# A decoder layer on one core: seven block products in the down projection of three token blocks, DeltaNet scalings moved to ScalarE, and two changes to the order of the work

## The chip, the cores and the metric

One core of a Trainium2 chip runs the whole program. The metric is the device time of one execution, in microseconds (us); lower is better. The kernel before was timed in three runs: median 2986.15 us, from 2983.44 to 2987.88.

The core has a matrix engine (TensorE, PE in the profile; its weight loads are listed apart as PEld), VectorE (DVE), ScalarE (ACT), GpSimd (POOL), and SyncE (SP), whose queue issues every transfer of this kernel.

## The reference, cut to what matters

```python
def decoder_layer(x, ...):
    y = parallel_mixer(rms_norm(x, norm_mix), ...)      # Conformer convolution | gated DeltaNet, then w_out
    x = x + y
    x = x + memory_attend(rms_norm(x, norm_mem_q), mem_k, mem_v, w_mq, w_mo)
    x = x + swiglu(rms_norm(x, norm_ffn), w_gate, w_up, w_down)
    return x, ...

def swiglu(h, w_gate, w_up, w_down):
    return (jax.nn.silu(h @ w_gate) * (h @ w_up)) @ w_down
```

There is one layer, a prompt of 2048 tokens, eight single decode tokens, a model width of 1024 and an FFN width of 2816. Everything is float32. The down projection multiplies a 2048x2816 activation by a 2816x1024 weight.

## The kernel before, in words

**Layout.** Channels lie on the 128 partitions and tokens along the free dimension. The prompt is cut into four blocks of 512 tokens (`NB`, `TB`). The FFN width is 22 tiles of 128 channels (`NF`), taken as 11 pairs (`NG`); the model width is 8 tiles (`KC`). The decode tokens ride along: in the FFN they are added to block 2 (`DEC_F`), whose token halves are therefore 260 wide and not 256.

**Float32 in three passes.** A number is split into a rounded upper part and the rest. `three` issues three matmuls for one weight tile: upper times upper, upper weight times lower operand, lower weight times upper operand. Each matmul instruction brings its own weight load.

**Weights.** `WS` streams them. `load` issues a transfer into one of 11 `raw` tiles (`NRAW`); `split` makes a `w` tile of two parts from it, with a copy on ACT and a subtraction on POOL or DVE, into one of 6 slots (`NW`). `engine` chooses POOL if the planner's clock says that POOL will be free soon enough, else DVE. The plan (`plan`) lists in advance which tile is used when. A tile that is already split in DRAM (`sums`) is loaded straight into its slot.

**The FFN of a block.** `ffn_steps` lists the steps. For each tile `f` of the FFN width, gate and up are computed together as a 2x2 block product over two halves of the contraction and two halves of the tokens, with seven products instead of eight (`Q1 P5 P6 Q2 Q3 Q7 P4`): each product is 12 matmuls, 256 tokens wide (260 in block 2). Four of the seven weights are sums of blocks. Block 0 computes the sums, splits them and writes them to DRAM (`sums`); blocks 1 to 3 load them from there. Products share PSUM banks by a letter (x, y, z; tiles `fx`, `fy`, `fz`): a later product adds to what an earlier one left in the bank, and an engine reads the bank in between. `ff_split` multiplies the two results and splits the product on ACT and DVE into an `act` tile (`ff`); there are 22 such tiles (`NACT`), and 14 of them hold the operands of gate and up during a block.

**The down projection.** `down(g, j)` takes a pair of FFN tiles `g` and two of the eight output tiles: 2 outputs x 2 tiles x 3 passes = 12 matmuls of 512 tokens (tile `dn`), from one weight tile; in block 2, 24 matmuls of 260. Four such steps, one before `P4` and three after it, finish a pair. Each output is then added to the residual `x` on DVE (`add_x`, `add_half`). Block 2 leaves three pairs (`HOLD`) to `rest`, which runs while the operands of block 3 are made; block 3 ends in `last`, in two halves of the tokens, followed by the final norm.

**The rest.** Before the FFNs, the first 1200 us or so hold the input projection, the convolution and the DeltaNet of all blocks (`dn_front`, `dn_chain`), the memory keys and values, and the output and attention parts of blocks 0 and 1; those of blocks 2 and 3 come after the FFNs of blocks 0 and 1. `square_gemm` does the projections with a square weight. For `w_out` in block 0 it begins with two output tiles at once, in the other blocks with four, and takes the remaining output tiles one by one.

**What sets the order.** Two planners. While the program is written down, `Sched` and `Clock` run a list of lanes against estimated costs; here POOL or DVE is chosen, and tiles get their slots. `Engine` estimates each ACT, DVE and POOL instruction. Then `Tape.order` puts every instruction of every engine in its final order: at each point the free engine takes, of its instructions whose inputs are ready by the estimated times, the one that is due first. That order is fixed; the engines then run it and wait for each other by semaphores.

Every instruction is issued by a helper, so all rows of the profile name one line (L469); rows are told apart by their tiles.

## Time and profile before

| | |
|---|---|
| median of three runs | 2986.15 us |
| the profiled execution | 2990.62 us |
| its span, first to last instruction | 2988.8 us |
| mean granted TensorE clock | 0.994 of full speed |
| matmul instructions | 18972 |
| PE busy | 2932.8 us (98%) |
| DVE busy | 2002.1 us (67%) |
| POOL busy | 1478.9 us (49%) |
| ACT busy | 1312.1 us (44%) |
| moved by DMA | 593.89 MB, 199 GB/s |

A row of a group names the line, the engine, the operation, the tile written and the tiles read, and how many; then the busy time of all, the mean of one in ns, and the idle time before them with what ended it. A row of the timeline gives the start, the length and the same names. Since matmuls are pipelined, the length of one (about 280 ns at 256 columns) is not its cost in a run: that is the distance from the start of one run to the start of the next, divided by the number of matmuls. Rows of the windows view give each engine's busy time in a stretch, the granted clock, the DMA engines' busy share and the rate.

### The profile page before, as it was taken

The numbers are of one execution on the slowest core, as the hardware profiler recorded it, in microseconds if no ns is written. First come the engines' busy times: TensorE is split into PE (matmuls) and PEld (weight loads), VectorE is DVE, ScalarE is ACT, GpSimd is POOL, SyncE is SP. The second block draws the span as 40 slices with busy tenths as digits, with TensorE's granted clock in tenths as the row PEclk, the third lists the DMA queues.
The fourth block names the chain that finished last, engine by engine and source line by source line (L and its number), as shares of the span: only waits on it lengthen the run. The fifth ranks groups of instructions, "written<-read, shape, count | busy, mean of one in ns | idle before, by whom it ended". The sixth has DMA issues, their size and how long they took to land. (4 is left out here: it accounts for less than half of the span.)

```text
span 2988.8 us, 53327 instructions
## 1 busy us (share of the span) xinstructions
PE 2932.8 (98%) x18972; PEld 2609.6 (87%) x18972; DVE 2002.1 (67%) x4105; ACT 1312.1 (44%) x2672; POOL 1478.9 (49%) x1403
## 2 busy tenths in 40 slices
PE   9999999999999999999999999999999999999998
PEld 7998878887888887899988789988888999999997
DVE  8758897987755757998788974433675444664345
ACT  6533455444654344545544553333453233333233
POOL 3544554786554654457776124445413444344444
PEclk9999999999999999999999999999999999999999
DMA  6533425777663425766768767867526666666664
GB/s 213 157 102 99 138 93 173 256 236 249 222 222 117 131 82 195 234 196 212 268 252 268 247 216 244 268 220 241 185 91 227 208 226 215 212 239 220 216 224 136
DMA packets 361963, 593.89 MB, mean 199 GB/s; under 512 B 54017, under 2 KB 148545, under 8 KB 361681
## 3 DMA queue, kind: packets, MB, share of 16 engines
q1 hardware_dynamic: 361696, 590.47, 59.9%
q8 instruction: 151, 2.47, 0.3%
q14 instruction: 116, 0.94, 0.1%
HBM read 476.65 MB, written 114.27 MB: 198 GB/s over the span
## 5 line engine op out<-in xcount | busy, mean ns | idle before, releaser
L469 POOL TENSOR_TENSOR w<-raw,w 128x512 fp32r<-128x512 f32 x713 | 962.3, 1359 | 891.1 <-ACT w L469 842.3
L469 ACT ACTIVATE w<-raw 128x512 fp32r<-128x512 f32 x912 | 569.7, 631 | 905.2 <-PE fx L469 183.7
L469 PE MATMUL dn<-ff,w 128*128 128x512 f32 (+2 forms) x2688 | 518.1, 348 | 3.9 <-ACT ffs L469 2.6
L469 PEld LDWEIGHTS dn<-ff,w 128*128 128x128 f32 x2688 | 422.1, 188 | 64.7 <-ACT ffs L469 2.8
L469 PE MATMUL fy<-op,w 128*128 128x256 f32 (+1 forms) x3168 | 428.5, 283 | 4.7 <-DMA w<-sums 3.2
L469 PEld LDWEIGHTS fy<-op,w 128*128 128x128 f32 x3168 | 400.5, 189 | 10.4 <-DVE ffu L469 3.0
L469 PE MATMUL hd<-hT,w 128*128 128x512 f32 (+2 forms) x1920 | 396.7, 358 | 9.1 <-ACT w L469 5.9
L469 DVE SCALAR_TENSOR_TENSOR cacc<-cu,cw,cacc 128x512 f32<-128x512 f32 x480 | 358.2, 746 | 9.0 <-ACT cacc L469 3.8
L469 PEld LDWEIGHTS hd<-hT,w 128*128 128x128 f32 x1920 | 306.3, 190 | 54.6 <-ACT w L469 6.6
L469 DVE TENSOR_TENSOR x<-dn,x 128x512 f32<-128x512 f32 (+1 forms) x448 | 254.1, 571 | 129.2 <-PE dn L469 126.3
L469 PE MATMUL fz<-op,w 128*128 128x256 f32 (+1 forms) x2112 | 287.0, 283 | 1.0 <-DMA w<-sums 0.9
L469 PE MATMUL fx<-op,w 128*128 128x256 f32 (+1 forms) x2112 | 285.3, 283 | 1.0 <-DVE ffs L469 0.9
L469 PEld LDWEIGHTS fx<-op,w 128*128 128x128 f32 x2112 | 268.3, 189 | 7.8 <-issue 1.2
L469 PEld LDWEIGHTS fz<-op,w 128*128 128x128 f32 x2112 | 265.8, 189 | 3.7 <-issue 2.6
L469 POOL TENSOR_TENSOR sqj<-sqj,sqj 128x512 f32<-128x512 f32 (+1 forms) x98 | 134.9, 1376 | 255.7 <-ACT sqj L469 253.3
L469 DVE TENSOR_TENSOR w<-raw,w 128x512 fp32r<-128x512 f32 x199 | 167.2, 845 | 59.8 <-ACT w L469 55.8
L469 PE MATMUL sc<-w,hT 128*128 128x512 f32 x768 | 190.2, 399 | 3.2 <-DVE w L469 1.7
L469 PE MATMUL rg<-catS,w 128*128 128x512 f32 (+2 forms) x960 | 189.4, 353 | 0.0
L469 PE MATMUL rg<-pT,w 128*128 128x512 f32 x768 | 188.9, 399 | 0.4 <-ACT pT L469 0.4
L469 DVE TENSOR_TENSOR ffu<-fy,ffu 128x256 f32<-128x256 f32 (+1 forms) x176 | 74.3, 422 | 164.1 <-PE fy L469 163.7
L469 PEld LDWEIGHTS rg<-catS,w 128*128 128x128 f32 x960 | 154.4, 188 | 24.4 <-ACT jn L469 0.2
L469 PEld LDWEIGHTS sc<-w,hT 128*128 128x128 f32 x768 | 141.6, 188 | 37.5 <-DVE w L469 2.6
(378 smaller groups left out, 4089.6 us busy)
## 6 DMA issues: line engine op xcount, KB each, us to landing
w<-sums SPq DMA_DIRECT2D x296, 512.0 KB, 4.4
raw<-in_w_gate_dram SPq DMA_DIRECT2D x192, 256.0 KB, 3.2
sums<-w SPq DMA_DIRECT2D x88, 512.0 KB, 4.1
raw<-in_w_down_dram SPq DMA_DIRECT2D x176, 256.0 KB, 3.3
raw<-in_w_up_dram SPq DMA_DIRECT2D x118, 256.0 KB, 3.0
raw<-in_w_in_dram SPq DMA_DIRECT2D x96, 256.0 KB, 3.0
raw<-in_w_out_dram SPq DMA_DIRECT2D x64, 256.0 KB, 3.1
raw<-wk SPq DMA_DIRECT2D x64, 256.0 KB, 2.8
```

The costliest lines, as they stand in the source:

```text
L469: fn(*args, **kw)
```

## The change

**Seven products in the down projection** of blocks 1 to 3, for the first ten of the eleven pairs. A pair of FFN tiles, the outputs `j` and `j + 4`, and the two token halves make a 2x2 block product. `downs(g, j)` does two pairs at once: seven products of 2 pairs x 3 passes = 6 matmuls each, 256 (260) wide, so 42 matmuls and four weight tiles a step. `pair_split` makes the sums of the activations on DVE and splits them into four `act` tiles for a pair (3.5 tiles' worth of elements) where there were two. In block 1 `sums_down` makes the sums of the weights with four 128-column instructions on POOL or DVE and writes both weight tiles unsplit to DRAM (`dsums`); blocks 2 and 3 load them and split them. The columns of `w_down` are laid out for this on the host. The steps stand in pairs around `P4` of two FFN tiles in four. In block 2, `x` now holds the decode columns beside the others, so that one addition does both.

```diff
+DS_B = 1
+NDS = 5
+DS_AT = ((1, 0), (1, 1), (2, 0), (2, 1))
...
+    def ffn_steps_ds(b):
+        steps = []
+        for f in range(NF):
...
+            steps += [("Q2", f), ("Q3", f), ("Q7", f)]
+            units = [[], []]
+            for g in range(NDS - (b == NB - 2)):
+                for j, (df, end) in enumerate(DS_AT):
+                    if f == min(4 * g + 4 + df, NF - 1):
+                        units[end].append(("downs", g, j))
+            early = not units[0] + units[1] and f + 1 < NF
+            if early:
+                steps.append(("Q1", f + 1))
+            steps += units[0] + [("P4", f)] + units[1]
...
+    def downs_plan(b, g, j):
+        if b > DS_B:
+            for n in range(2):
+                for p in (2 * g, 2 * g + 1):
+                    plan.append(("dsums", "s", (p, j), n))
+            return
+        raws = {}
+        for p in (2 * g, 2 * g + 1):
+            for n in (1, 0):
+                raws[p, n] = plan.raw("dma", "w_down", "h", (p, j), n)
...
+        def sums_down(self, at, r0, r1):
+            (a11, a12, s1, s2), (s3, s4, a22, a21) = ([r[:, n * P : (n + 1) * P] for n in range(4)] for r in (r0, r1))
+            eng = self.engine(2600.0)
+            for out, x, y, op in (
+                (s1, a21, a22, ALU.add), (s2, s1, a11, ALU.subtract), (s3, a11, a21, ALU.subtract), (s4, a12, s2, ALU.subtract)
+            ):
+                eng.tensor_tensor(out=out, in0=x, in1=y, op=op)
+            p, j = at
+            dma(wsrc["dsums"][p, j, 0], r0)
+            dma(wsrc["dsums"][p, j, 1, :, : 3 * P], r1[:, : 3 * P])
...
+        def pair_split(p):
+            (u1, s1), (u2, s2) = prod.pop(2 * p), prod.pop(2 * p + 1)
+            half = lambda t, n: t[:, n * w : (n + 1) * w]
+            yield [u2, s2]
+            V.tensor_tensor(out=u2, in0=u2, in1=s2, op=ALU.mult)
+            V.tensor_tensor(out=half(s2, 1), in0=half(u2, 1), in1=half(u1, 1), op=ALU.subtract)
+            V.tensor_tensor(out=half(u1, 1), in0=half(u1, 1), in1=half(u1, 0), op=ALU.subtract)
+            V.tensor_tensor(out=half(s2, 0), in0=half(u2, 1), in1=half(u1, 1), op=ALU.subtract)
+            V.tensor_tensor(out=half(s1, 0), in0=half(u2, 0), in1=half(s2, 0), op=ALU.subtract)
+            for n, (src, wd) in enumerate(((u1, 2 * w), (u2, 2 * w), (s2, 2 * w), (s1, w))):
+                yield ("act", 1)
+                a = act("fo")
+                A.activation(out=a[:, 0, :wd], in_=src[:, :wd], func=AF.Copy)
+                yield a
+                V.tensor_tensor(out=a[:, 1, :wd], in0=src[:, :wd], in1=a[:, 0, :wd].bitcast(F32), op=ALU.subtract)
...
+        def downs(g, j):
+            ps_ = (2 * g, 2 * g + 1)
+            S.until(lambda: all((p, n) in hx for p in ps_ for n in range(4)), "ff")
+            wts, bk = {}, {}
+            for n, at, (x, h), t, m, half in (
+                (0, 0, (0, 0), "x", j, 0), (0, 1, (1, 0), "y", j, 0), (0, 2, (0, 1), "z", j + 4, 1), (0, 3, (2, 0), "x", j, 1),
+                (1, 1, (1, 1), "z", j, 1), (1, 0, (2, 1), "x", j + 4, 1), (1, 2, (3, 0), "x", j + 4, 0),
+            ):
...
+                first = t not in bk
+                if first:
+                    bk[t] = pm("d" + t, (P, w))
+                pt = bk[t]
+                for p in ps_:
+                    wt = wts[n, p]
+                    three([pt], wk(wt, 0, at), wk(wt, 1, at), hx[p, x], [(h * w, (h + 1) * w)], first and p == ps_[0], p == ps_[1], True)
+                    tick()
...
+                V.tensor_tensor(out=xs[m][:, lo:hi], in0=pt, in1=xs[m][:, lo:hi], op=ALU.add)
```

The letter in `downs` is the PSUM bank: the seven products go to x, y, z, x, z, x, x in this order, and after each one DVE reads its bank into the residual.

**Small DeltaNet scalings on ScalarE**: five DVE instructions become ACT instructions, and the last of them becomes four.

```diff
-        V.tensor_copy(
-            out=t16.rearrange("p (i j) -> p i j", j=16), in_=w16[:, 0:256].rearrange("p (j i) -> p i j", i=16)
+        A.activation(
+            out=t16.rearrange("p (i j) -> p i j", j=16), in_=w16[:, 0:256].rearrange("p (j i) -> p i j", i=16), func=AF.Copy
...
-        V.tensor_scalar(out=u1[64:P], in0=pu[64:P], scalar1=-1.0, scalar2=None, op0=ALU.mult)
+        A.activation(out=u1[64:P], in_=pu[64:P], func=AF.Copy, scale=-1.0)
...
-        V.tensor_copy(out=W[0:64, :, 64:P], in_=pu)
+        A.activation(out=W[0:64, :, 64:P], in_=pu, func=AF.Copy)
...
-            V.tensor_scalar(out=vv, in0=pc[:, 1, :], scalar1=brk[:, c : c + 1], scalar2=None, op0=ALU.mult)
+            A.activation(out=vv, in_=pc[:, 1, :], func=AF.Copy, scale=brk[:, c : c + 1])
...
-        V.tensor_tensor(out=osc, in0=po, in1=bc(fc, 2, [P, NT, DK]), op=ALU.mult)
+        for c in range(NT):
+            A.activation(out=osc[:, c, :], in_=po[:, c, :], func=AF.Copy, scale=fc[:, c : c + 1])
```

**Shared port in the list's clock**: the first planner's clock now lets a POOL instruction and a DVE instruction with two SBUF inputs start only one after the other.

```diff
+            port = self.name == "pool" or self.name == "dve" and sum(a.space != bass.MemoryType.PSUM and elems(a) > 1 for a in ins) > 1
+            if port:
+                self.clock.at[self.name] = max(self.clock.at[self.name], self.clock.port)
+            t = self.clock.run(self.name, ns, ins, out)
+            if port:
+                self.clock.port = t + ns
```

**Paired output tiles**: `square_gemm` begins `w_out` with two output tiles in every block, and the weight is loaded in the form that block 0 used.

```diff
-        square_plan("w_out", CAT, b == 0)
+        square_plan("w_out", CAT, True)
...
-        n0 = 2 if dec else 4
+        two = w == "w_out"
+        n0 = 2 if two else 4
```

More of the change, by code (lines that the diff above doesn't have):

```diff
@@ L975, in split, with split_down @@
             self.used(k)
+        def split_down(self, j, k, r, t):
+            _, _, at, n = plan[j]
+            wd = TB - n * P
+            if plan.raws[k][2] == "h" and n == 0:
+                self.sums_down(at, r, self.raw[k - 1])
+            A.activation(out=t[:, 0, :wd], in_=r[:, :wd], func=AF.Copy)
+            self.engine().tensor_tensor(out=t[:, 1, :wd], in0=r[:, :wd], in1=t[:, 0, :wd].bitcast(F32), op=ALU.subtract)
+            self.tiles[j] = t
+            self.sp += 1
+            self.used(k)
+        def sums_down(self, at, r0, r1):
[8 more added lines that the diff above has]
+            dma(wsrc["dsums"][p, j, 1, :, : 3 * P], r1[:, : 3 * P])
         def ready(self, k):
+            if 0 <= k < self.ld and plan.raws[k][2] == "h" and plan.raws[k][4] == 0 and C.when([self.raw[k - 1]]) > S.vt:
+                return False
             return k < 0 or k < self.ld and C.when([self.raw[k]]) <= S.vt
@@ L2234, in square_gemm @@
         for m in range(n0):
-            if m == n0 - 1:
-                S.until(lambda: any(C.bank_free(t) < 1e12 for t in ("mm", *others())), "fourth bank")
-            pts.append([pm("rg", (P, hi - lo), others() if len(spans) * m + k > 2 else []) for k, (lo, hi) in enumerate(spans)])
+            pts.append([])
+            for k, (lo, hi) in enumerate(spans):
+                lent = lambda: others() if len(spans) * m + k > 2 else []
+                S.until(lambda: any(C.bank_free(t) < 1e12 for t in ("mm", *lent())), "fourth bank")
+                pts[m].append(pm("rg", (P, hi - lo), lent()))
         for n_, kc in enumerate(order):
-            if not dec:
+            if not two:
                 wt = ws.get(w, "r", kc, 0)
@@ L2252, in square_gemm @@
                 tick()
-            if not dec:
+            if not two:
                 ws.free(1)
@@ L2725, in rest @@
         def rest():
-            for g in range(NG - HOLD, NG):
-                for j in range(KC // 2):
-                    down(g, j)
+            for j in range(KC // 2):
+                downs(NDS - 1, j)
+            for j in range(KC // 2):
+                down(NG - 1, j)
             if b == DEC_F:
```

100 lines of the change are left out of this document (79 added, 21 removed).

## The prediction, made before the change was run

> **What bounds the kernel now.** I read the page's busy times first, then the stages in the windows view, then what PE waited for.
>
> ```profile
> PE 2932.8 (98%) x18972; PEld 2609.6 (87%) x18972; DVE 2002.1 (67%) x4105; ACT 1312.1 (44%) x2672; POOL 1478.9 (49%) x1403
> ```
> ```profile
> 300.00:600.00 300.00, 296.17 (x1673) 245.37 (x1673) 263.33 (x567) 148.78 (x313) 165.21 (x197) 0.99 0.51 165
> 600.00:900.00 300.00, 287.21 (x1706) 246.59 (x1705) 213.97 (x407) 161.94 (x320) 193.01 (x185) 0.99 0.71 231
> ```
> ```profile
> 1230.00:1600.00 370.00, 366.52 (x2632) 335.97 (x2631) 316.96 (x584) 180.92 (x390) 251.24 (x229) 1.00 0.69 234
> ...
> 1786.00:2118.00 332.00, 329.00 (x2293) 301.71 (x2292) 146.28 (x257) 117.78 (x223) 157.96 (x120) 1.00 0.74 247
> ...
> 2288.00:2598.00 310.00, 308.65 (x2564) 308.11 (x2563) 148.05 (x429) 99.60 (x193) 135.76 (x99) 1.00 0.70 228
> ...
> 2640.00:2957.00 317.00, 315.80 (x2241) 295.85 (x2240) 135.12 (x233) 99.51 (x191) 140.61 (x104) 1.00 0.67 224
> ```
>
> In a windows row the columns after the length are PE, PEld, DVE, ACT, POOL, the granted clock, the DMA share and GB/s. The last four rows are the FFNs of blocks 0 to 3. In those of blocks 1 to 3 PE is busy for 329.00 of 332, 308.65 of 310 and 315.80 of 317 us, at the full clock, while DVE, ACT and POOL are under half busy. So matmul time sets the end, and a matmul removed there is a matmul's time gained until something else is late. What PE waited for, in the whole span, says how little that is now:
>
> ```profile
> PE fy L469 <- DMA w<-sums: 3.2, 4, 1.5
> ...
> PE dn L469 <- ACT ffs L469: 2.6, 1, 2.6
> ```
>
> The busy time of a pipelined group is not its cost, so I take the pace from starts of neighbouring runs in the timeline, once for 512 columns and once for 260:
>
> ```profile
> 1518.47 2.95 PE L469 MATMUL dn<-ff,w 128*128 128x512 f32 x12
> 1521.26 1.58 PE L469 MATMUL fy<-op,w 128*128 128x256 f32 x12
> 1522.68 8.55 PE L469 MATMUL dn<-ff,w 128*128 128x512 f32 x36
> 1531.07 1.58 PE L469 MATMUL fx<-op,w 128*128 128x256 f32 x12
> 1532.49 1.58 PE L469 MATMUL fz<-op,w 128*128 128x256 f32 x12
> ```
> ```profile
> 2309.72 3.11 PE L469 MATMUL dn<-ff,w 128*128 128x260 f32 x24
> 2312.67 1.60 PE L469 MATMUL fy<-op,w 128*128 128x260 f32 x12
> 2314.11 8.80 PE L469 MATMUL dn<-ff,w 128*128 128x260 f32 x72
> 2322.75 1.62 PE L469 MATMUL fx<-op,w 128*128 128x260 f32 x12
> 2324.20 1.61 PE L469 MATMUL fz<-op,w 128*128 128x260 f32 x12
> ```
>
> From 1522.68 to 1531.07, 36 matmuls of 512: 8.39 us, 233 ns each. From 1531.07 to 1532.49, 12 of 256: 1.42 us, 118.3 ns each. So half the columns cost 51% of the time, with a weight load in each. Of 260: 8.64 / 72 = 120.0 ns (down), 1.44 / 12 and 1.45 / 12 = 120.4 ns (gate and up).
>
> **The matmuls.** Blocks 1 and 3: a pair took 2.79 + 8.39 = 11.18 us; ten pairs 111.8 us. Now there are 5 groups x 4 steps x 42 = 840 matmuls of 256: 840 x 0.1183 = 99.4 us. Saved: 12.4 us in each. Block 2: a pair took 2.95 + 8.64 = 11.59 us, ten 115.9; now 840 x 0.1204 = 101.1. Saved: 14.8 us. Sum: **39.6 us** less on PE.
>
> One rule of the Trainium skill speaks against this: "TensorE: Matmul & The Clock Gate", section "Back-to-back issue gap", says that in a stream with a weight load for each matmul both set the spacing, about 81 ns at 128 columns and 131 ns at 512. On a straight line between these, an estimate, 256 columns cost 98 ns, and a block's down projection would go from 480 x 131 = 62.9 to 840 x 98 = 82.3 us. The trace has 233 and 118.3 ns, and does not bear it out.
>
> **A bank that is read between products.** In a step, product 7 adds to bank x, which product 6 has just filled and DVE must have read; and product 6 needs bank x read after product 4, with only product 5 (6 x 0.118 = 0.71 us) between. No row of before shows a product waiting like that; the nearest turn from PE to DVE is in a DeltaNet chain:
>
> ```profile
> 1481.61 0.38 PE L469 MATMUL pch<-S,kT 128*128 128x128 f32 x2
> ...
> 1482.15 0.34 DVE L469 SCALAR_TENSOR_TENSOR chr<-pch,neg,dn 128x128 f32<-128x128 f32 x1
> ```
> ```profile
> L469 DVE TENSOR_TENSOR x<-dn,x 128x512 f32<-128x512 f32 x74 | 51.0, 690 | 39.4 <-PE dn L469 38.6
> L469 DVE TENSOR_TENSOR ffu<-fy,ffu 128x256 f32<-128x256 f32 x42 | 17.8, 423 | 46.9 <-PE fy L469 46.9
> L469 DVE TENSOR_TENSOR ff<-ffu,ff 128x512 fp32r<-128x512 f32 x21 | 17.1, 814 | 1.5 <-ACT ff L469 1.4
> L469 DVE TENSOR_TENSOR ffu<-ffu,ffs 128x512 f32<-128x512 f32 x21 | 14.5, 692 | 2.0
> ```
>
> PE ends at 1481.99, DVE starts 0.16 us later; a 256-column read is 0.42 us; with as much again for the way back, 0.74 us. Over 5 x 4 x 3 = 60 steps that is 44 us if nothing fills it, and 0 if something does. `Tape.order` gives PE the earliest-due ready matmul, and beside nearly every step stands `P4`, the next `Q1` or another step with a bank of its own. I take 3 us, near the filled end, since the products of gate and up share banks in the same way and the FFNs lose 1 to 3 us.
>
> **Weight tiles.** A step of 2.79 us used one weight tile; the new step of 42 x 0.118 = 4.97 us uses four (two of 512 columns, two of 384). POOL does the subtraction today. Block 1 also makes the sums.
>
> ```profile
> L469 POOL TENSOR_TENSOR w<-raw,w 128x512 fp32r<-128x512 f32 x119 | 158.6, 1346 | 174.5 <-ACT w L469 169.6 <-DMA w<-sums 3.1
> ```
> ```profile
> L469 POOL TENSOR_TENSOR w<-raw,w 128x512 fp32r<-128x512 f32 x95 | 131.0, 1389 | 44.4 <-ACT w L469 43.5 <-DMA cat<-catc 0.4
> L469 POOL TENSOR_TENSOR raw<-raw,raw 128x512 f32<-128x512 f32 x52 | 76.8, 1484 | 28.8 <-DVE raw L469 6.9 <-DVE lnx L469 6.8 <-DMA raw<-in_w_up_dram 5.3
> ```
> ```profile
> L469 DVE TENSOR_TENSOR w<-raw,w 128x512 fp32r<-128x512 f32 x72 | 68.3, 954 | 13.5 <-ACT w L469 12.5 <-DMA raw<-in_w_up_dram 0.8
> L469 DVE SCALAR_TENSOR_TENSOR cacc<-cu,cw,cacc 128x512 f32<-128x512 f32 x83 | 61.5, 741 | 0.2
> ```
>
> The first row is block 1's FFN, the other four block 0's. Block 1 after: POOL, if it did all, 119 - 40 + 40 = 119 tiles x 1.346 = 160 us, 40 of 384 x 1.01 = 40, and 160 sums of 128 columns x 0.34 (a quarter of 1.346) = 54: 254 us of some 320. DVE with two SBUF inputs: 10 pairs x (2 x 0.692 + 4 x 0.423 + 3.5 x 0.814) = 59 us, and what it has there for cat and the decode tokens, some 17 tiles x 0.814 = 14. Together 327 us of 320: over 100%, if the two exclude each other. Block 0 is the nearest row: POOL 251.24 and, from these two DVE rows alone, 129.8, together 381 of 370 us, and PE lost 370 - 366.52 = 3.5 us. I take 3 us in block 1 and 1 each in blocks 2 and 3, which make no sums (DVE's 148 and 135 us rise by 10 x (4 x 0.423 + 1.5 x 0.814) = 29, POOL's by 40 x 1.01). Bounds: 0, and 2 us for each of block 1's ten bursts, 20.
>
> **Transfers.** Block 1's FFN again:
>
> ```profile
> DMA packets 33017, 82.03 MB, mean 247 GB/s; under 512 B 3666, under 2 KB 3666, under 8 KB 32988
> ...
> q1 hardware_dynamic: 32988, 81.64, 73.6%
> ...
> w<-sums SPq DMA_DIRECT2D x80, 512.0 KB, 4.4
> raw<-in_w_down_dram SPq DMA_DIRECT2D x40, 256.0 KB, 2.7
> ```
>
> It gets 40 writes of 256 KB and 40 of 192 KB, 18.4 MB: 100.4 MB in 320 us, 314 GB/s, and 0.736 x 332 x 100.4 / 82 / 320 = 93% of the DMA engines. The weight loads become 80 of half the size; the writes stand in SP's queue ahead of later loads, and wait there for the sums. No long stretch shows such a share. I take 3 us, bounds 0 and 15. Blocks 2 and 3 read 18.4 instead of 10.5 MB: about 80%, nothing.
>
> **DeltaNet, port, paired tiles.**
>
> ```profile
> L469 DVE TENSOR_SCALAR chv<-pch,brk x64: 329/342/352, 185.6 to 1485.5; 128x128 f32<-128x128 f32 x64
> ```
> ```profile
> L469 DVE TENSOR_TENSOR osc<-po,fc x16: 669/690/693, 232.0 to 1495.3; 128x512 f32<-128x512 f32 x16
> ```
> ```profile
> L469 ACT ACTIVATE lny<-lnq,vcol x64: 438/456/475, 540.7 to 1479.8; 128x128 f32<-128x128 f32 x64
> ```
>
> DVE is relieved of 64 x 0.342 + 16 x 0.690 = 33 us and some smaller ones; ACT, at 149 to 181 us of 300 to 370, gets 128 x 0.456 = 58. PE is idle for 3.8 and 12.8 us in the two mixer windows; gains or losses (an ACT step is 0.11 us longer, in 64 links of chains with slack) stay within 6 us either way. I take 0. The port in the clock only re-deals POOL and DVE; the paired tiles move no matmul in or out, but want the concatenated input in half the time, with 20 us of down projection ahead of it. 0, within the same 6.
>
> **Sum.** 39.6 - 3 - 5 - 3 = 28.6 us. The profiled execution goes from 2990.62 to 2962.0, its span from 2988.8 to 2960.2. The median of the runs is 4.5 us below the profiled one, so I expect 2986.15 - 28.6 = **2957.5 us**.
>
> **Rivals.**
>
> *Bank x stands in the way* (slower). Place: products 6 and 7 of each step. If DVE is mid-instruction when a product ends, half of 0.814 us comes on top, for both: 0.41 + 0.74 + 0.41 = 1.56 us a step, 94 us in all, 3040. Bare turns give 44: 2991. It decides from 39.6 / 60 = 0.66 us a step. For: DVE takes its work in order, and has 29 us more a block. Against: the filling work above. Between its ends, some 3000 us.
>
> *Block 1 cannot be fed.* Weight tiles at their upper bound, 20 + 2, and transfers 5 over what I took: 39.6 - 3 - 22 - 8 = 7 us gained at these ends, 17 half-way to the forecast's: about 2974. For: 327 of 320 us, and 93% of the DMA engines. The Trainium skill, "SBUF — State Buffer", section "Who interferes with whom", makes POOL and a DVE instruction with two SBUF inputs exclude each other for the whole instruction, which would make the 327 a floor and give this case. Against, by block 0's rows: 381 of 370 us and 3.5 us lost, so these busy times hold waits, or work was shared out better.
>
> *All comes back.* Bursts of steps in blocks 2 and 3 starve as well, and the mixer loses its 6 us: 2986.
>
> *Narrow matmuls cost more than half.* From 111.8 / 840 = 133 ns nothing is gained; at the trace's 118.3 only a cost of a run of 6, which no row shows, could do that. This, like the page's pace, would end near 3000.
>
> **How the numbers follow.** Forecast, own range 2946 to 2968: 0.57. Block 1 not fed, 2968 to 2980: 0.20. Under 2946, with the mixer gaining: 0.04. All back: 0.08. Bank x: 0.10. Narrow matmuls: 0.01. A measurement of this kernel can tell 0.2%, 6 us, from no change; so faster 0.81, same 0.08, slower 0.11. The range takes the forecast, most of the fed case, and the better side down to the full 39.6 and a few us: 2942 to 2981.
>
> **What would show it.** Matmuls from 18972 to 18972 + 2 x 360 - 120 = 19572, PE busy down by about 39. Block 1's FFN near 320 us, PE idle there at most 12; DMA share near 0.93. No wait of PE for DVE `x` of more than 3 us in all: tens of us there mean bank x; long waits for ACT or POOL `w`, or for DMA `raw`, in block 1 mean it was not fed. A pace of the new runs of over 0.71 us for 6 would break the first term; a gain under 6 us or over 45 would break the sum.

## The result, and the profile after

The changed kernel is slower, by 0.7%: a median of 3012.57 us (six runs, 3003.67 to 3020.6) against 2987.78 us (six runs, 2983.44 to 2996.62) for the kernel before on the same chip, a ratio of 1.0073 (95% interval 1.0059 to 1.0087). Forecast were 2957.5 us. The profiled execution of the changed kernel took 3020.6 us, the longest of the six, with a span of 3018.9 (before 2988.8) and a mean granted clock of 0.988 (before 0.994).

The page's busy times, the FFNs of blocks 1, 2 and 3 in the windows view, and PE's waits:

```profile
PE 2924.9 (97%) x19572; PEld 2630.6 (87%) x19572; DVE 2143.9 (71%) x4204; ACT 1441.6 (48%) x3023; POOL 1589.9 (53%) x1584
```
```profile
1775.00:2135.00 360.00, 338.84 (x2635) 321.40 (x2634) 224.05 (x428) 149.01 (x290) 200.80 (x236) 0.97 0.84 281
2311.00:2617.00 306.00, 303.33 (x2498) 301.30 (x2498) 169.79 (x336) 124.17 (x244) 164.44 (x130) 1.00 0.78 255
2661.00:2990.00 329.00, 321.90 (x2684) 318.62 (x2684) 190.15 (x371) 129.71 (x255) 183.53 (x146) 1.00 0.76 247
```
```profile
PE fz L480 <- DMA w<-sums: 18.9, 16, 3.0
PE fy L480 <- DMA w<-sums: 8.6, 10, 2.0
```

All 19572 matmuls are there, as forecast. But PE is idle for 21 of 360 us in block 1's FFN, where it was idle for 3 of 332, and the clock there is 0.97 on average. PE now waits 27.5 us for `w<-sums`: the weight tiles of gate and up that come from DRAM already split and go straight into a slot. The matmuls on the tiles that the change adds (`dx`, `dy`, `dz`) wait for no DVE, and 1.0 us in all for ACT; their weight loads (PEld) wait 1.0 us in all for DVE `x`.

One late load in block 1, from the timeline (start, length, engine; PE and SP's queue only):

```profile
1963.63 0.38 SPq L480 DMA_DIRECT2D w<-sums  x1
...
1965.82 0.87 PE L480 MATMUL fy<-op,w 128*128 128x256 f32 x6
...
1966.53 0.39 PE L480 MATMUL podd<-vtl,pb 128*64 128x512 f32 x1
...
1966.76 0.86 PE L480 MATMUL fy<-op,w 128*128 128x256 f32 x6
...
1970.65 0.80 PE L480 MATMUL fz<-op,w 128*128 128x256 f32 x2 [3.03 <-DMA w<-sums]
```
```profile
1969.00:1976.00 7.00, 5.34 (x20) 4.20 (x21) 1.44 (x6) 1.01 (x2) 2.28 (x3) 0.54 0.50 179
```

The semaphore that ended this wait belongs to the load issued at 1963.63. PE wanted it 4.0 us later, when `fy` ended at 1967.62, and got it 7.0 us after the issue. The windows row of the 7 us from 1969 shows the second half of the bill: a mean granted clock of 0.54. The clock fell while the stall still lasted; from 1970.65, where PE goes on, to 1976.00 it is 0.50.

The 26 waits for such loads, read one by one in the same way, mostly begin with a slot that came free late. In 20 of them (19.8 of 27.4 us) SP had been waiting for PE's last use of the slot and issued the load as soon as the slot was free. In the other 6 (7.6 us, the one above among them) the slot was already free, and the load stood behind earlier entries of SP's queue.

From the starts of the first `fx` of a block and of the last `rg` matmul of block 3's output, the timeline gives lengths that can be compared between kernels (us). "FFN 0 and 1" runs from the first `fx` to that last `rg`; it is taken as one, because the decode tokens' attention slides to and fro between its parts. The 94 us between it and block 2 hardly change (94.0 to 94.5) and are left out. Lengths are of one profiled execution each, ratios of all runs. A profiled execution lies between 12.6 us below the median of its runs (`turns_nw7`) and 9.9 above it (`addall`); the changed kernel's lies 8.0 above, so differences of a few us between two rows say nothing.

| kernel | up to FFN 0 | FFN 0 and 1 | block 2 | block 3 to the end | ratio to before (95%) |
|---|---|---|---|---|---|
| before | 1186.8 | 996.3 | 353.2 | 358.4 | |
| after | 1189.5 | 1026.8 | 350.3 | 357.9 | 1.0073 (1.0059 to 1.0087) |
| forecast | 1186.8 | 983.9 | 338.4 | 346.0 | (before its 11 us of losses) |
| small_only | 1186.6 | 1003.2 | 351.9 | 360.2 | 1.0010 (0.9999 to 1.0021) |
| seven_only | 1192.3 | 1004.4 | 350.5 | 356.1 | 1.0034 (1.0018 to 1.0050) |
| ds2 | 1185.6 | 1000.8 | 374.4 | 358.0 | 1.0076 (1.0052 to 1.0099) |
| spread | 1188.8 | 1036.6 | 351.6 | 355.1 | 1.0090 (1.0063 to 1.0118) |
| dmaplan | 1183.6 | 1034.6 | 353.3 | 360.8 | 1.0137 (1.0115 to 1.0160) |
| nw6_small | 1207.0 | 1005.2 | 352.3 | 357.8 | 1.0081 (1.0061 to 1.0101) |
| nw7 | 1204.3 | 991.9 | 346.2 | 351.4 | 0.9992 (0.9981 to 1.0004) |
| nw7_dec14 | 1198.9 | 999.8 | 345.6 | 351.5 | 1.0002 (0.9990 to 1.0014) |
| before_pair_nw7 | 1205.8 | 997.0 | 350.7 | 357.8 | 1.0045 (1.0029 to 1.0061) |
| seven_pair_nw7 | 1212.3 | 998.7 | 344.8 | 350.7 | 1.0007 (0.9990 to 1.0024) |
| presum | 1189.0 | 1013.2 | 352.4 | 358.8 | 1.0027 (1.0015 to 1.0039) |
| presum_nw7 | 1200.3 | 987.5 | 346.7 | 351.8 | 0.9959 (0.9944 to 0.9973) |
| nowrite_nw7 | 1201.9 | 984.2 | 346.4 | 349.9 | 0.9947 (0.9928 to 0.9966) |
| restmix_nw7 | 1202.6 | 994.9 | 346.2 | 349.9 | 0.9988 (0.9975 to 1.0002) |
| turns_nw7 | 1194.2 | 992.0 | 347.7 | 348.8 | 0.9995 (0.9984 to 1.0006) |
| both_nw7 | 1197.3 | 990.9 | 346.1 | 350.6 | 0.9992 (0.9980 to 1.0004) |
| addall | 1198.5 | 1009.5 | 357.9 | 350.6 | 1.0037 (1.0025 to 1.0049) |
| addall_nw7 | 1203.3 | 988.8 | 354.0 | 347.4 | 0.9981 (0.9969 to 0.9993) |

So the profiled executions miss the 39.6 us of matmuls by 69.7: 42.9 in FFN 0 and 1 (30.5 longer instead of 12.4 shorter), 11.9 in block 2, 11.9 in block 3, and 3 up to FFN 0 and between the blocks. By the medians the miss is smaller: 3012.57 for 2957.5, 55 us. The first two columns belong together, since work moves between them: `nw6_small`, explained below, is 17.5 us longer than the changed kernel in the first and 21.6 shorter in the second.

### The profile page after: what moved, and what is told of

Read it like the earlier page. It is cut to its first block, busy times and chain, and to the rows that moved or that the text cites. A ratio compares the mean times of both kernels' runs of the same rounds, so it can differ in the third digit from the quotient of the medians.

```text
span 3018.9 us, 55688 instructions
## 1 busy us (share of the span) xinstructions
PE 2924.9 (97%) x19572; PEld 2630.6 (87%) x19572; DVE 2143.9 (71%) x4204; ACT 1441.6 (48%) x3023; POOL 1589.9 (53%) x1584
## 5 line engine op out<-in xcount | busy, mean ns | idle before, releaser
L480 POOL TENSOR_TENSOR w<-raw,w 128x512 fp32r<-128x512 f32 (+1 forms) x750 | 993.2, 1334 | 758.2 <-ACT w L480 678.0
L480 ACT ACTIVATE w<-raw 128x512 fp32r<-128x512 f32 (+1 forms) x1032 | 624.0, 617 | 858.0 <-PE fy L480 108.7
L480 PE MATMUL hd<-hT,w 128*128 128x512 f32 (+2 forms) x1920 | 388.6, 355 | 6.5 <-ACT w L480 5.8
L480 PE MATMUL fz<-op,w 128*128 128x256 f32 (+1 forms) x2112 | 295.0, 285 | 19.1 <-DMA w<-sums 18.9
L480 PE MATMUL fx<-op,w 128*128 128x256 f32 (+1 forms) x2112 | 293.7, 282 | 0.3 <-ACT ffs L480 0.3
L480 DVE TENSOR_TENSOR w<-raw,w 128x512 fp32r<-128x512 f32 (+1 forms) x282 | 229.7, 822 | 68.9 <-ACT w L480 64.3
L480 PE MATMUL dx<-fo,w 128*128 128x256 f32 (+1 forms) x1440 | 216.0, 286 | 0.3
L480 PEld LDWEIGHTS dx<-fo,w 128*128 128x128 f32 x1440 | 187.6, 189 | 3.3 <-DVE x L480 1.0
L480 PE MATMUL dn<-ff,w 128*128 128x512 f32 (+2 forms) x768 | 171.1, 375 | 6.3 <-DVE xd L480 3.6
L480 PEld LDWEIGHTS rg<-pT,w 128*128 128x128 f32 x768 | 142.7, 190 | 34.3 <-ACT pT L480 1.9
```

The lines of the kernel that those rows point to most:

```text
L480: fn(*args, **kw)
```

## The experiments

Three theories stood at the start. **L** (lead): six weight slots turn over too fast, so a load straight into a slot lands too late, in all three blocks. **T** (throughput): block 1 has more for POOL, DVE and the DMA engines than fits. **M**: the small parts disturb the mixer and the decode tokens' attention. Ratios are to the kernel before, on the same chip.

### Which part of the change costs

`small_only` is the kernel before with the DeltaNet scalings, the port and the paired tiles; `seven_only` has the seven products alone.

> The kernel before with the three small parts alone (DeltaNet scalings on ScalarE, the port in the first planner's clock, w_out begun with two output tiles), no seven products. Theory L (lead: the steps of the down projection turn the six weight slots over faster, so that the loads of the gate and up sums come late) and theory T (throughput: block 1's FFN has too much for POOL, DVE and the DMA engines) both expect the kernel before within 5 us, 2983 to 2993, since in the changed kernel's trace the stages ahead of block 1's FFN end 3 us later. Theory M (the small parts re-order the mixer and push the decode attention into block 1) expects 10 us or more over the kernel before.

> The seven products alone, the three small parts undone. L and T expect what the whole change gave, 3005 to 3020, with some 27 us of PE waiting for loads of sums. M expects most of the 39.6 us of matmul time to show: under 2975, and the decode attention spread over the attention of block 2 as in the kernel before.

Measured: 2996.7 us (1.0010) and 3003.49 (1.0034), beside 2992.16. The small parts alone cost 3 us (0 to 6 by the interval), not the 10 or more of M, so they are not the cause by themselves. The seven products alone already lose, with waits for `w<-sums` of 11.7 and 8.6 us. But they lose less than L and T expected (3005 to 3020): put on top of them, the small parts cost 1.0073 - 1.0034 = 0.0039, 12 us (5 to 18). What the small parts do there was not taken apart.

### Moving the making of the sums, and spreading the steps

`ds2` leaves block 1 as it was, so that block 2 makes the sums. `spread` puts one step at a time instead of pairs.

```diff
-DS_B = 1
+DS_B = 2
```
```diff
-DS_AT = ((1, 0), (1, 1), (2, 0), (2, 1))
+DS_AT = ((1, 0), (2, 0), (3, 0), (4, 0))
```

> The whole change, but block 1's FFN is done as before and the seven products begin in block 2, which makes the sums (the constant DS_B is 2). Block 1's FFN with its output part took 42.6 us more than its matmuls allow, blocks 2 and 3 12 each. T expects that block 2 now pays for making the sums as block 1 did, 20 us or more: about 3000. L expects block 2 to lose near 12 to 18 and block 3 12: 2985 to 2993. If block 1's loss came of the decode attention that is crowded there, block 2 pays no more than 12: 2980 to 2987.

> The whole change with six slots, but one step of the down projection at each of four FFN tiles ahead of P4, where there were two around P4 at each of two tiles. L expects little, within 6 us of the whole change's 3012: between the load of a sum and its use there still lie four short-lived tiles of a step. If it is the bunching of two steps, which POOL and the DMA engines cannot feed, the waits fall by half and the time by 10 us or more.

Measured: 3017.06 (1.0076) and 3022.25 (1.0090). Block 2 grows by 21.2 us as soon as it makes the sums; 9.2 us of that is one wait of PE for ACT `ff` in what it leaves to the mixer. So the making costs wherever it stands, as T had it; but the whole is dearer than either theory said (about 3000, or 2985 to 2993), and `w<-sums` still makes PE wait 21.5 us. Spreading the steps brings the waits for `w<-sums` down from 27.5 to 16.5 us and the time not at all: the interval reaches from below the changed kernel's 1.0073 to above it. Block 2 stays at 351.6. So the bunching is not what costs the time, and the sum of these waits alone does not give it either.

### A seventh slot, and its controls

`nw7` is the changed kernel with one more weight slot. The memory for it comes from two other pools; `nw6_small` takes those away and keeps six slots. `before_pair_nw7` gives the same seven slots and pools to the kernel before (with the paired tiles, which this memory plan needs), and `seven_pair_nw7` adds the seven products to that, without the DeltaNet scalings and the port.

```diff
-NW = 6
-NT2 = 28
+NW = 7
+NT2 = 27
...
-NRAW = 11
+NRAW = 10
```

> The whole change with seven weight slots instead of six; room is made by ten raw tiles instead of eleven and 27 temporary tiles instead of 28. L expects PE's waits for loads of sums to fall from 27 to under 10 us, and the time by 15 us or more, to 2990 or less. T expects the same time within 5 us, 3007 to 3018, with the same waits, since a slot adds no engine and no bandwidth.

> The changed kernel with its six weight slots, but with the smaller other pools that the run with seven slots needed (10 raw tiles for 11, 27 work tiles for 28). It separates the slot from those pools. Theory L (lead: a split tile is loaded straight into its slot, and with six slots it lands too late): the slot is all that helped, so this stays at 1.007 to 1.012 of the kernel before, with PE's waits for DMA w<-sums over 18 us. Rival (fewer raw tiles hold the loads of w_down back, so that the loads of split tiles land sooner): near 1.000, waits under 10 us.

> The kernel before with seven weight slots, ten raw tiles and 27 temporary tiles, and the paired output tiles, without seven products in the down projection. L expects the kernel before within 5 us: there the loads of sums were late in six cases of 264 only, so a seventh slot has nothing to win. If the seventh slot were worth 15 us or more here too, it would be a gain of its own and say nothing of the seven products.

> Seven weight slots, ten raw tiles and 27 temporary tiles, the seven products and the paired output tiles, but neither the DeltaNet scalings on ScalarE nor the port in the first planner's clock. L expects the waits for loads of sums under 10 us as in the run with all parts, and since the seven products alone were some 9 us faster than the whole, 2980 to 2987 where the kernel before has 2992. T expects 3000 or more.

Measured: 2989.58 (0.9992), 3012.78 (1.0081), 3005.95 (1.0045) and 2994.15 (1.0007). PE's waits and the FFNs of blocks 1 to 3 with seven slots, and then the waits of `nw6_small` and of `before_pair_nw7`:

```profile
PE fy L480 <- DMA w<-sums: 3.6, 3, 2.2
...
PE fz L480 <- DMA w<-sums: 3.3, 4, 1.2
```
```profile
1776.00:2114.00 338.00, 327.29 (x2631) 313.08 (x2630) 225.08 (x426) 148.38 (x290) 206.51 (x238) 1.00 0.87 295
2290.00:2593.00 303.00, 303.00 (x2498) 301.99 (x2497) 164.57 (x334) 122.60 (x243) 164.32 (x130) 1.00 0.80 256
...
2637.00:2960.00 323.00, 321.80 (x2694) 319.90 (x2694) 183.05 (x376) 129.34 (x258) 183.57 (x146) 1.00 0.78 251
```
```profile
PE fz L480 <- DMA w<-sums: 14.0, 18, 1.9
PE fy L480 <- DMA w<-sums: 7.4, 11, 1.6
```
```profile
PE fy L469 <- DMA w<-sums: 0.8, 1, 0.8
```

The slot alone, at the same pools, is worth 1.0081 - 0.9992 = 0.0089, some 27 us (20 to 33 by the two intervals). The waits for `w<-sums` fall from 21.4 to 6.9 us, PE has no idle time left in block 2's FFN, and the clock is back at 1.00 in block 1's. L stands. The two other runs missed what was expected of them (2983 to 2993 or so, and 2980 to 2987). The place is up to FFN 0, where the smaller pools, the likely reason, cost some 19 us (1205.8 against 1186.8); the kernel before with small pools and six slots was not run. From FFN 0 on, the kernel before hardly gains from the slot: 2 us (1802.0 to 1799.7). With seven slots and those pools the change is worth 1.0045 - 0.9992 = 0.0053, 16 us, of which the seven products bring 1.0045 - 1.0007 = 0.0038. The pools alone show no loss in the changed kernel: `nw6_small` ends level with it (1.0081 and 1.0073).

The lead can be worked out from the pace of the prediction's rows. A pair of FFN tiles took 14 products of 12 matmuls (14 x 1.42 us) and 11.18 us of down projection, 31.1 us, from 14 + 4 = 18 weight tiles: 1.73 us each, so six slots turn over in 10.4 us. Now it takes 19.9 us and two steps of 4.97, 29.8 us, from 14 + 8 = 22 tiles: 1.36 us each, 8.1 us for six slots and 9.5 for seven. Inside a pair of steps a tile lasts 4.97 / 4 = 1.24 us, and six slots 7.5. From this must be taken the use of the tile (1.4 us, or longer if another step stands between), the wait in SP's queue, and the landing: 8.1 - 1.4 = 6.7 us are left, an estimate, where the load shown above took 7.0 from issue to use.

### An order that counts on slower transfers, and a later place for the decode tokens

`dmaplan` tells the second planner that transfers take 1.35 times as long; its second addition, 0.6 us more to land, changed a number that isn't read afterwards, so only the factor was tried. `nw7_dec14` moves the output of the decode tokens' attention two FFN tiles back.

```diff
-                dma_at = max(dma_at, s + 1100) + ns
+                dma_at = max(dma_at, s + 1100) + 1.35 * ns
```
```diff
-DEC_O = (1, 12)
+DEC_O = (1, 14)
```

> The changed kernel with six slots, and the second planner told longer transfers: 1.35 times the time each takes on the queue and 0.6 us more to land. Nothing else is changed; only the order can differ. If the late loads come from an order that counts on 3.5 us where 4.4 to 5.2 are measured, PE's waits for DMA w<-sums fall by half (to 10 to 14 us) and the whole to 0.999 to 1.004. Rival (six slots give no order that is better): the waits stay over 20 us and the whole at 1.005 to 1.009.

> Seven slots, and in addition the due place of the decode tokens' attention in block 1 two FFN tiles later (f = 14 for 12). If its rush ahead of f = 12 is part of block 1's loss, block 1 gets 3 to 10 us shorter than with seven slots alone (410 to 417 us from its start to the start of block 2's FFN less the output part, 420.0 before), and the whole lies at 0.996 to 0.998. Rival (that work only takes its own time wherever it stands): within 3 us of seven slots alone, 0.999.

Measured: 3029.25 (1.0137) and 2991.29 (1.0002). PE's waits with `dmaplan`:

```profile
PE fx L481 <- ACT ffu L481: 8.4, 17, 1.1
PE fx L481 <- POOL w L481: 6.9, 9, 1.7
PE fy L481 <- DVE ffu L481: 6.5, 11, 1.6
...
PE fz L481 <- DMA w<-sums: 4.6, 7, 1.2
```

The waits for `w<-sums` did fall, to less than expected (4.6 us, not 10 to 14), but the kernel became slower still, which neither forecast had: now PE waits for other tiles and results. That the six slots hold these up is a reading of the rows, not tested. This order, at least, does not supply the missing slot. The decode tokens' attention (`podd` in the rows above), which is hurried along beside the stalls, costs nothing that a later place would give back.

### What of the making of the sums costs

`presum` and `presum_nw7` leave the making out (blocks 1 to 3 load tiles of `w_down` where the sums belong, so the result is not the layer's); `nowrite_nw7` adds the sums up but doesn't write them (loads in blocks 2 and 3 read `w_down` in their place).

```diff
-            dma(wsrc["dsums"][p, j, 0], r0)
-            dma(wsrc["dsums"][p, j, 1, :, : 3 * P], r1[:, : 3 * P])
```

> The whole change with six slots, without the making of the weight sums: block 1 takes the tiles of w_down as they are in the place of the sums, loads them as blocks 2 and 3 do, and neither adds nor writes; blocks 2 and 3 load the same tiles. The arithmetic of the down projection in blocks 1 to 3 is left out in so far; every matmul, split and load of tiles stays. T (throughput) expects block 1 to come near what its matmuls allow, a loss under 5 us instead of some 35, so 2985 or less for the whole. L (lead) expects block 1 to lose as much as blocks 2 and 3 do, about 12 us, and the decode attention's 7 us moved into it: 2990 to 2998, with at least 15 us of PE waiting for loads of sums left.

> Seven slots, and block 1 neither adds nor writes the sums of the weights: blocks 1 to 3 load tiles of w_down as they are where the sums belong, so a part of the arithmetic is left out. If lead and the making of the sums are two separate losses, this is some 14 us below seven slots alone: 0.994 to 0.996, with block 1 at 400 to 408 us. Rival (both hit the same resource in block 1, and curing one cures most of the other): 0.997 to 0.999, block 1 at 412 us or more.

> Seven slots; block 1 adds up the sums of the weights and uses them, but doesn't write them, and blocks 2 and 3 load tiles of w_down in their place, so a part of the arithmetic is left out there. It divides the 10.7 us that making the sums cost with seven slots (from 0.9992 to 0.9959) between the additions and the writes. If the writes and their share of the queue are what costs: 0.995 to 0.997, block 1 at 407 to 412 us. If the additions on POOL and DVE are: 0.998 to 1.000, block 1 at 416 us or more.

Measured: 3001.21 (1.0027) with six slots, 2979.84 (0.9959) and 2976.01 (0.9947) with seven. With six slots that is slower than either theory had it (2985 or less, or 2990 to 2998), with 17.4 us of waits for `w<-sums` left. Lead and making are two losses: leaving out the making is worth 0.0046 with six slots and 0.0033 with seven. And it is the writes: without them, with all the additions still made in block 1, the gain is 0.0045, 13 us (7 to 20). Block 1's transfers (1780 to 2110 us) with the writes and seven slots, and then without the writes:

```profile
DMA packets 47834, 97.48 MB, mean 295 GB/s; under 512 B 5315, under 2 KB 19011, under 8 KB 47798
...
q1 hardware_dynamic: 47798, 97.01, 86.5%
...
w<-sums SPq DMA_DIRECT2D x84, 512.0 KB, 5.2
...
dsums<-raw SPq DMA_DIRECT2D x36, 256.0 KB, 5.8
```
```profile
DMA packets 39193, 83.47 MB, mean 253 GB/s; under 512 B 4328, under 2 KB 14452, under 8 KB 39156
...
q1 hardware_dynamic: 39156, 83.00, 76.3%
...
w<-sums SPq DMA_DIRECT2D x84, 512.0 KB, 4.5
```

The last number of a row of issues is the median time to landing. With the writes a split tile lands 5.2 us after its issue, without them 4.5; before it was 4.4. The queue was not full in either case, but each load came later, on top of a lead that was already short. Writes are not the only thing that lengthens a landing: blocks 2 and 3 of the changed kernel, which write no sums, have 4.9 and 5.2 us, and block 1 of `presum` 5.0. So that the writes cost 13 us is shown; by which path they do, the landing or the places that they take in SP's queue, is not. What POOL did meanwhile in `nowrite_nw7`, by groups, in block 1:

```profile
L480 POOL TENSOR_TENSOR w<-raw,w 128x512 fp32r<-128x512 f32 x72 | 99.9, 1392 | 56.6 <-ACT w L480 53.0 <-DVE x L480 2.7
L480 POOL TENSOR_TENSOR raw<-raw 128x128 f32<-128x128 f32 x110 | 69.0, 633 | 32.7 <-DMA raw<-in_w_down_dram 26.3 <-DVE x L480 2.8 <-DVE ffu L480 2.7
...
L480 POOL TENSOR_TENSOR raw<-raw,raw 128x128 f32<-128x128 f32 x37 | 22.7, 614 | 0.0
```

POOL made 147 of the narrow additions in 91.7 us, and it still stood idle for 338 - 212 = 126 us. PE was idle for 4 of the 338 us, where before it was idle for 3 of 332.

### What was still missing in blocks 2 and 3

With seven slots the loads land in time, but blocks 2 and 3 are 7 us shorter each, not 14.8 and 12.4. Two places were left in the trace of `nw7`: a wait in what block 2 leaves to the mixer, with a slow stretch behind it,

```profile
PE dn L480 <- DVE xd L480: 3.6, 2, 2.4
```
```profile
2627.00:2634.00 7.00, 5.36 (x23) 4.85 (x24) 6.79 (x19) 3.90 (x7) 1.79 (x2) 0.54 0.12 43
```

and the turn of a bank. In the timeline of the changed kernel, runs of 6 on bank x and z follow each other in block 3:

```profile
2726.08 0.87 PE L480 MATMUL dz<-fo,w 128*128 128x256 f32 x6
2726.78 0.96 PE L480 MATMUL dx<-fo,w 128*128 128x256 f32 x6
2727.58 0.87 PE L480 MATMUL dz<-fo,w 128*128 128x256 f32 x6
2728.29 0.95 PE L480 MATMUL dx<-fo,w 128*128 128x256 f32 x6
2729.08 1.59 PE L480 MATMUL fy<-op,w 128*128 128x256 f32 x12
```

The planner has already changed the order of the list: x and z alternate. A run that meets a fresh bank takes 0.70 us (2726.08 to 2726.78), one on bank x with one product since the last 0.80 and 0.79; the second run on z, at 2727.58, takes 0.71. `restmix_nw7` takes the last group of block 2 and the old-way pair in turn; `turns_nw7` changes the order of the products; `both_nw7` does both.

```diff
             for j in range(KC // 2):
                 downs(NDS - 1, j)
-            for j in range(KC // 2):
                 down(NG - 1, j)
```
```diff
-                (0, 0, (0, 0), "x", j, 0), (0, 1, (1, 0), "y", j, 0), (0, 2, (0, 1), "z", j + 4, 1), (0, 3, (2, 0), "x", j, 1),
-                (1, 1, (1, 1), "z", j, 1), (1, 0, (2, 1), "x", j + 4, 1), (1, 2, (3, 0), "x", j + 4, 0),
+                (0, 0, (0, 0), "x", j, 0), (0, 2, (0, 1), "z", j + 4, 1), (0, 3, (2, 0), "x", j, 1), (0, 1, (1, 0), "y", j, 0),
+                (1, 0, (2, 1), "x", j + 4, 1), (1, 1, (1, 1), "z", j, 1), (1, 2, (3, 0), "x", j + 4, 0),
```

> Seven slots, and what block 2 leaves to the mixer (the last group of seven products and the old-way pair) is taken in turn, a step of the one and a step of the other, where it was four and then four. With seven slots PE waited there 3.6 us for DVE xd before two of the old-way steps, and ran 6.8 us at half the clock right after. If that stall is why block 2 gains 7 us and not 14.8, block 2 (start of its FFN to start of block 3's) falls from 346.2 to about 339 us and the whole to 0.996 to 0.998. Rival (DVE is late there whatever the order, since it makes the operands of block 3 in the same place): 344 us or more, the whole unchanged at 0.999 to 1.000.

> Seven slots, and the seven products of a step in the order of banks x z x y x z x where it was x y z x z x x, with the same sums, banks and weight tiles: between any two products on bank x lies one on another bank. With seven slots the matmuls of dx and dz in block 3 run at 124 and 122 ns where fx, fy, fz run at 119, some 3 us a block in all. If the short turn of a bank is the cause, dx falls to 119 to 120 ns, blocks 2 and 3 get 1 to 3 us shorter each and the whole lies at 0.997 to 0.999. Rival (one product between is as short a turn as none, and x now has three such): no change, or 1 to 2 us a block longer.

> Both of the edits before at once, as the best version that the runs point to: if both work, 0.994 to 0.997 of the kernel before; if neither, 0.999 to 1.001.

Measured: 2989.86 (0.9988), 2991.57 (0.9995) and 2986.97 (0.9992): none differs from `nw7` by more than the noise, and the rivals hold. With the steps mixed PE waits for DVE `x` in the same place (`both_nw7`: 4.2 us before `dz`); DVE makes the operands of block 3 there and is late in either order. The timeline of `turns_nw7` shows the turns unchanged:

```profile
2711.07 0.94 PE L480 MATMUL dx<-fo,w 128*128 128x256 f32 x6
2711.84 0.94 PE L480 MATMUL dz<-fo,w 128*128 128x256 f32 x6
2712.62 0.88 PE L480 MATMUL dx<-fo,w 128*128 128x256 f32 x6
```

From 2711.07 to 2712.62 two runs still take 0.77 and 0.78 us. One product between two on a bank does not fill the turn, and the list's new order put no more between them than the planner had done before.

### A version without writes

If the writes cost and the additions don't, each block can make its own sums. `addall_nw7` does so with seven slots, `addall` with six; both compute the whole layer.

```diff
-        if b > DS_B:
+        if b < DS_B:
             for n in range(2):
...
-            p, j = at
-            dma(wsrc["dsums"][p, j, 0], r0)
-            dma(wsrc["dsums"][p, j, 1, :, : 3 * P], r1[:, : 3 * P])
```

> Seven slots, and nothing is written: each of blocks 1 to 3 loads its quarter of w_down and adds up the sums itself, so the arithmetic is whole. If the writes were the cost of making the sums and the additions are nearly free beside the matmuls, block 1 is at 408 to 413 us, blocks 2 and 3 as with seven slots (346 and 352 us), and the whole lies at 0.994 to 0.996 of the kernel before. Rival (the additions do cost POOL and DVE time where they come on top of the splits, 54 us of POOL a block by the estimate in the prediction): blocks 2 and 3 lose 3 to 10 us each, 0.997 to 1.002.

> The same with the six slots and pools of the changed kernel. It tells whether the lead that six slots give is too short only because the new loads and writes slow the transfers. If so, w<-sums lands in 4.4 us as before, PE's waits for it fall below 10 us and the whole lies at 0.995 to 0.999. Rival (the slots turn over too fast in themselves, since a step takes four of them): waits of 15 us or more and 1.001 to 1.005.

Measured: `addall_nw7` 2987.04 us beside 2990.8 (0.9981, 0.9969 to 0.9993), `addall` 3002.58 (1.0037). The first is the only whole version whose interval lies below 1: faster than the kernel before by 0.2%. Its windows: block 1's FFN, block 2's FFN, what block 2 leaves, and block 3's FFN; and its longest wait:

```profile
1783.00:2110.00 327.00, 323.06 (x2608) 308.65 (x2607) 221.89 (x423) 148.32 (x287) 207.39 (x236) 1.00 0.78 253
...
2298.00:2600.00 302.00, 302.00 (x2495) 300.78 (x2494) 205.90 (x401) 122.67 (x242) 178.72 (x219) 1.00 0.72 225
2600.00:2645.00 45.00, 33.21 (x250) 31.84 (x249) 42.04 (x107) 20.66 (x37) 9.61 (x7) 0.85 0.41 132
2650.00:2960.00 310.00, 310.00 (x2602) 309.37 (x2602) 225.08 (x431) 125.07 (x247) 179.55 (x225) 1.00 0.71 228
```
```profile
PE dn L480 <- DVE x L480: 10.9, 3, 7.4
```

The FFNs of blocks 2 and 3 have no idle PE at all, and block 3 is 11.0 us shorter than before, of 12.4 forecast. So the additions hide beside the matmuls there. Where they don't is what block 2 leaves: DVE is busy for 42.04 of 45 us, PE waits, and the clock is 0.85; this gives back what block 2 gained (354.0 us, 346.2 in `nw7`). So the whole lies in the rival's range (0.997 to 1.002), and block 2 loses what the rival said, but block 3 nothing. It was not tried to relieve DVE there. `addall`, with six slots, waits 7.8 us for `w<-sums` (6.0 and 1.8), within what was expected if only the transfers were at fault, but the whole lies where the rival put it: a single wait of 10.4 us for ACT `ff` in what block 2 leaves, and 13 us more in FFN 0 and 1 than before, in an execution 9.9 us above the median. Without any writes the slot is still worth 1.0037 - 0.9981 = 0.0056, 17 us, of which those waits are 7.8. Where six slots lose the rest was not taken apart.

## Why the prediction was wrong

**The step that failed** is the pair of terms "Weight tiles" ("I take 3 us in block 1 and 1 each in blocks 2 and 3") and "Transfers" ("I take 3 us", and for blocks 2 and 3 "nothing"): 8 us together. Measured in their place: 27 us for the missing slot (1.0081 to 0.9992) and 13 us for the writes (0.9992 to 0.9947), 40 us. Both terms were sized by throughput: so much POOL and DVE time, so large a DMA share of the stage. None of these was full: POOL was idle for 159 of block 1's 360 us, and the DMA share was 0.84. What ran out was the time between the moment when a slot comes free and the moment when its tile is wanted, which no sum of busy times shows. These 40 us are not the whole miss: with the slot and without the writes the ratio is 0.9947, where the forecast is 2957.5 / 2986.15 = 0.9904. Of these last 13 us some 6 are bank x, an estimate, below; the cause of the others stays open. It was not the new tiles that came late either, but those of gate and up that were there before. The text says that a step uses four tiles where it used one, with 6 slots; it did not go on to divide the slots by the pace.

**The matmuls.** Right in the stage where it can be seen by itself: 19572 instructions, and block 3 is 11.0 us shorter in `addall_nw7`, of 12.4. In `nowrite_nw7` the FFN stages are 12.1, 6.8 and 8.5 us shorter than before, 27.4 of 39.6, though it is 15.1 us longer up to FFN 0, and a part of the 12.1 may be work that moved there. "PE busy down by about 39" was a bad sign to look for: it fell by 7.9 only (2932.8 to 2924.9). Busy time is longer at half the clock, and a run's modelled end hides short gaps; how much each does was not measured.

**Bank x.** 3 us were taken for all blocks. A short turn costs 0.08 or 0.09 us. A step has three on x and one on z, a block 80: 7 us if nothing filled one. In block 3 of `nw7` the starts within the runs of `dx` and `dz` lie 124 and 122 ns apart on average for 118.3, so 320 x 5.7 + 160 x 3.7 ns = 2.4 us in the 16 steps that stand there: about 3 a block, and 3 times the term. The rival with that name, 44 to 94 us through waits for DVE, is refuted: PE's waits have none for DVE before these tiles, and their weight loads 1.0 us.

**Weight tiles, POOL's part.** The additions were put at 0.34 us on POOL, a quarter of a 512-column one; they took 0.63. "327 of 320 us" was too low, then, and the end did not depend on it.

**Transfers.** The share in block 1 was forecast at 93%; it was 84%, in a longer stage. "The writes stand in SP's queue ahead of later loads" named the writes, and 13 us stand where 3 were taken; that SP's queue is the place is not shown.

**DeltaNet, port, paired tiles.** 0 was taken, within 6; `small_only` has 3, with 0 inside its interval. Beside the seven products with six slots, though, the small parts cost 12 us (5 to 18), which the term had at nothing; with seven slots the changed kernel is no slower than `seven_pair_nw7`, which lacks the scalings and the port (0.9992 and 1.0007).

**The rivals.** "Block 1 cannot be fed" came nearest by name, but was about POOL and DVE, priced at 2974 us, and would have left blocks 2 and 3 their gain. "All comes back" named starving in blocks 2 and 3, and had the smaller half of it. No rival priced a load that lands too late, though the prediction itself shows a row of four such waits before the change. "Narrow matmuls" is refuted by the 0.70 us of a run of 6.

**Half the clock.** No term of the sum had it. After the 3.0 us stall PE ran for at least 5.35 us at 0.50, which is 2.7 us of work lost on top of it. The mean clocks bound the whole: 3018.9 x 0.012 = 36 us against 2988.8 x 0.006 = 18, so at most some 18 of the 69.7 us, and less, since part of the slow time falls into the stalls themselves.

## What to carry to other kernels

A change that takes more tiles out of the same number of slots has to be sized by lead: the number of slots times the time that a tile lasts, less its use, against the measured time from issue to landing. Do this for the loads that go straight into a slot, whether or not the change touches them. A result that can be made again from data at hand may be cheaper than one that is written and read back, even if the queue has room: here the writes cost 13 us, with the DMA engines at 0.87 of their time, and the additions that took their place were hidden in the FFNs of blocks 2 and 3.

## What the runs showed of the hardware

Landing time differs well short of a full queue, and the queue's share alone does not give it: a 512 KB load landed in 4.4 us at 73.6% of the DMA engines (block 1 before), in 4.5 at 76.3% (`nowrite_nw7`) and in 5.2 at 86.5% (`nw7`), but also in 5.2 at 75.9% (block 3 of the changed kernel). A POOL addition of 128 columns took 0.63 us where one of 512 took 1.39, so a quarter of the columns cost nearly half. And a stall of PE of some 3 us (3.03 in the changed kernel, 3.6 in two waits close together with seven slots) went with half the granted clock for some microseconds: 0.50 from 1970.65 to 1976.00 in the first case, a mean of 0.54 over 7 us in the second.
